# Two holds on early side work in a decoder block: squares of x's rows, and the first weights of the FFN

## The chip, the core and the metric

The kernel runs on one core of a Trainium2 chip. A core has five engines, each with its own instruction queue that is worked through in order: TensorE (PE in the profile, its weight loads PEld), VectorE (DVE), ScalarE (ACT), GpSimdE (POOL) and SyncE (SP), which here mostly issues DMAs. [...] The metric is the device time of one execution in microseconds.

## The reference, cut to what matters

One layer of a hybrid decoder, for x of 2048 rows by 1024 columns in float32:

```
hn   = rmsnorm(x, norm1_g)
u_pool, q, k, v = split(hn @ w_in)             # 512 columns each, 8 heads of 64
y_pool = ((mean of the last 2, 4, 8, 16 rows) - u_pool) @ pool_w * pool_scale
z = q k^T / 8, strictly causal;  log_a = log_sigmoid(z) + sum over later keys of log_sigmoid(-z)
y_attn = exp(log_a) @ v
h  = x + concat(rmsnorm(y_pool), rmsnorm(y_attn)) @ w_out
h  = h + relu(rmsnorm(h, norm2_g) @ w_up) ** 2 @ w_down      # 4096 hidden columns
y  = rmsnorm(h, final_g)
```

## The kernel before

The 2048 rows are treated as four blocks j = 0 to 3 of 512 rows; a tile holds 128 features by 512 rows. A float32 product is made from three passes in a reduced format: each operand is split into a high and a low part, `split` (L147 to L151), by a copy on ACT (L150) and a subtraction on DVE (L151), and `products` (L176 ff.) issues three matmuls per 128 features (L182 to L184). Weights come by DMA in the tile `raw` and are split five granules ahead of their use (`hl`, in `weights`, L167 ff.). A "chunk" is one such product of 128 output features by 512 rows over all 1024 inputs: 24 matmuls into one PSUM tile `pd`, of which there are two. What then takes the result out of `pd` is the chunk's evacuation.

The program has four stages in a row. The **front** runs for blocks 0 and 1 and again for 2 and 3: input projections, the pooling branch and the attention units, interleaved. For columns of v, `keep_v` (L488) copies `pd` to `vf`, for block 0 by a multiplication on DVE (L491) and for the others by a copy on ACT (L493), and PE transposes `vf` into `ptv` (L496). Beside this, `row_sums` (L382) makes the sums of squares that block 1 to 3's first norm needs: a quarter of a block's rows (512 KB) comes by DMA into the one tile `rlast` (L390), ACT squares it and sums along the row (L388), and only then the next quarter's DMA is issued. `sum_rows` (L395) takes one such step; in the front's second half it is noted once per chunk or two chunks.

The **output stage** (`tail`) multiplies by w_out, eight chunks c per block. `add_acc` (L878) adds `pd` to x on DVE (L881), sends the sum to memory as `hs` (L882) and notes its square for the second norm. At chunk 3 of the last block `begin_ffn` (L1605) opens the **FFN's** pools and takes the first step of `up`, a generator: it loads the first columns of w_up into `rb` (L986, 1 MB), makes weights from it (sums `rt` on DVE, L990 to L993, and splits `hw`), and makes the left operands (`make_left`: loads `sr`, 512 KB each, L1009, three buffers, so that load number i waits for the split of number i-3, and splits them into `sa`). The FFN uses a two-level fast matrix multiplication of seven products P1 to P7; in its first column PE does 12 matmuls each of P1 (tile `pY`), P2 (`pX`), P5 (`pZ`), then P6 and P7 (`pY` again). Before P6 can start, ACT copies P1's result out of `pY` (`p`, L1108). The **down** projection and the last norm follow.

The order of instructions on each engine isn't the order of the text: a scheduler puts the traced program in order by dependencies and a modelled timeline, and an instruction whose operands it takes to be ready early may stand far ahead of where it was written. A scope `tc.issue_after(ins)` forbids that: what is traced in it on the engine of `ins` is put behind `ins`. It adds no semaphore and binds no other engine. `last_split[0]` is the subtraction (DVE) of the weight split traced last, `done[1]` the evacuation of the chunk traced last, which is on DVE or ACT according to the chunk; for `add_acc` it is the addition on DVE.

Of the kernel before, what the change touches and what calls it, by code (L numbers as in the profile page):

```python
# [19 lines left out]
NT = S // T  # L20
# [25 lines left out]
def hymba_block(ctx: ExitStack, tc: tile.TileContext, xT, x_rows, gains, w_in, pool_w, w_out, w_up, w_down, out):  # L46
# [111 lines left out]
    raws, grans, last_split, last_mm, last_load = [], [], [None], [None], [None]  # L158
    done = [None, None]
# [145 lines left out]
    def make_h(j):  # L305
        return (hpb if j % 2 else hpa).tile([P, 2, T], F32R, tag="h", name="h", align_bytes=256)
# [18 lines left out]
    def step(n, emit, again=False):  # L325
        prog.append((n, emit, again))

    def note(emit):
        prog.append((0, emit, False))
# [53 lines left out]
    def row_sums(j):  # L383

        x = rlast.rearrange("p x t -> p (x t)")
        for b in range(TB + 1):
            if b:
                nc.scalar.activation(x, x, AF.Square, accum_out=sums1[:, j - 1, b - 1:b])  # L388
            if b < TB:
                nc.sync.dma_start(x, x_rows[j, b])  # L390
            yield

    row_steps = [iter(())] + [row_sums(j) for j in range(1, NT)]

    def sum_rows(j, n=1):  # L395
        for _ in range(n):
            next(row_steps[j])

    def norm1_rms(j):
        st[j]["ss"] = sums1[:, j - 1]  # L400
# [144 lines left out]
    def drained(j):  # L545
        while j not in finished:
            state["due"] = 0.0
            advance(0.1)
# [57 lines left out]
    def load_mix(j, n):  # L606
        st[j]["m"] = []
        for k in range(n):
            d = make_h(j)
            nc.sync.dma_start(d.bitcast(F32), mx[j][k].bitcast(F32))  # L610
            st[j]["m"].append((d[:, 0], d[:, 1]))

    def load_acc(j):
        acc = st[j]["acc"] = (bigp, accp, acc2p, acc3p)[j].tile([P, KD, T], F32, tag="big", name="acc")
        for k in range(0, KD, 2):
            nc.sync.dma_start(acc[:, k:k + 2], xT[j, :, k:k + 2])

    def tail(first):

        def root(j):  # L620

            if not (first and j < 2):
                drained(j)
                st[j]["todo"] = attn_norm(j, lambda: make_h(j))

        def mixes(j):
            load_mix(j, KD if first and j < 2 else 4)
            if "todo" in st[j]:
                st[j]["amix"] = st[j].pop("todo")()

        def begin(j):
            catch_up(len(later))
            st[j]["m"] += st[j].pop("amix", [])
            if j > 0:
                norm2(j - 1)
            if j == 2:
                sums_first()

        if first:
            note(to_out)  # L640
        else:
            note(lambda: (root(0), mixes(0), load_acc(0)))
        for j in range(NT):
            if j == 2 and first:
                note(to_last)
            note(lambda j=j: begin(j))
            for c in range(KD):
                if c == 0 and j == 0 and not first:
                    note(lambda: root(1))
                if c == 0 and j + 1 < NT:  # L650
                    note(lambda j=j: mixes(j + 1))
                if c == (2 if j == 0 else 4) and j + 2 < NT:
                    note(lambda j=j: root(j + 2))
                if c == 0 and j == 2:
                    note(lambda j=j: load_acc(j))
                if c == 4 and j in (0, 2):
                    note(lambda j=j: load_acc(j + 1))
                if c == 3 and j == NT - 1:
                    note(begin_ffn)
                wlist.append(w_out[c])  # L660
                step(2, lambda w, j=j, c=c: dense(j, "m", w, lambda ps: add_acc(j, c, ps)))

# [190 lines left out]
    def attn_norm(j, make=None):  # L853
        part = {}

        def load():

            if make:
                ol = [olp.tile([P, 2, T], F32, tag="ol", name="ol") for _ in range(2)]
            else:  # L860
                y = pa.tile([P, 4, T], F32, tag="yb", name="yb", bufs=1)
                ol = [y[:, 0:2], y[:, 2:4]]
            for i in range(2):
                nc.sync.dma_start(ol[i], os_[j][2 * i:2 * i + 2].rearrange("c p t -> p c t"))
            part.update({k: ol[k // 2][:, k % 2] for k in range(4)})

        if make:
            load()
        else:
            drained(j)  # L870
            later.append(load)
        return norm_parts(j, lambda k: part[k], ga, 4, make)
# [18 lines left out]
    def norm2(j):  # L891
        acc = [st[j]["acc"][:, k] for k in range(KD)]
        if j == 2:
            later.append(lambda: root_last(0, st[j]["sh"]))
        else:
            later_rms(st[j], "rh", lambda: st[j]["sh"], D)

        def put(k):
            nc.vector.scalar_tensor_tensor(acc[k], acc[k], g2[:, k:k + 1], st[j]["rh"], op0=ALU.mult, op1=ALU.mult)
        if j in PAIRS[0]:  # L900
            later.extend(lambda k=k: put(k) for k in range(KD))
# [12 lines left out]
    def sums_first():  # L914

        a, b = (st[j]["acc"] for j in PAIRS[0])

        def sums(c):
            lo, hi = slice(2 * c, 2 * c + 2), slice(4 + 2 * c, 6 + 2 * c)
            s1 = olp.tile([P, 2, T], F32, tag="sm", name="s1")  # L920
            nc.vector.tensor_tensor(s1, b[:, lo], b[:, hi], ALU.add)
            nc.vector.tensor_tensor(b[:, lo], a[:, lo], b[:, lo], ALU.subtract)
            s2 = olp.tile([P, 2, T], F32, tag="sm", name="s2")
            nc.vector.tensor_tensor(s2, s1, a[:, lo], ALU.subtract)
            for i, t in ((A11, a[:, lo]), (S2, s2), (A12, a[:, hi]), (S3, b[:, lo]), (S1, s1), (A22, b[:, hi])):
                nc.sync.dma_start(su[0][i][c], t)
            nc.vector.tensor_tensor(a[:, hi], a[:, hi], s2, ALU.subtract)
            nc.sync.dma_start(su[0][S4][c], a[:, hi])
        later.extend(lambda c=c: sums(c) for c in range(2))

    def up(pools, more):
# [49 lines left out]
        def load(q, m):  # L981
            if q and m % (NM // 2) == NM // 2 - 1:
                raw[q, m] = raw[0, m]
                return
            raw[q, m] = (rbb if m >= NM // 2 else rba).tile([P, 4, G, P], F32, tag="rb", name="rb")
            nc.sync.dma_start(raw[q, m], w_up[m])  # L986
# [9 lines left out]
        def make_weights(g):  # L996
            q, m, s = slots[g]
            which, i = what[s][1]
            if s == "P2":
                add_weights(q, m)  # L1000
            hl = hlp.tile([P, 2, G, P], F32R, tag="hw", name="hw", align_bytes=256)
            split((hl[:, 0], hl[:, 1]), (sums if which else raw)[q, m][:, i])
            ops[g] = hl
# [147 lines left out]
                    inner_sums(*waiting.pop(0))  # L1151

        load(*cols[0])
        make_weights(0)
        make_left(0, "P1")
        make_left(0, "P2")
# [9 lines left out]
        for g, (q, m, s) in enumerate(slots):  # L1166
# [7 lines left out]
            n = cols.index((q, m))  # L1174
# [19 lines left out]
            if g + UA < len(slots):  # L1194
                make_weights(g + UA)
                q2, m2, s2 = slots[g + UA]
                n = cols.index((q2, m2)) + 2
# [375 lines left out]
    def catch_up(n, stop=False):  # L1573
        for _ in range(n):
            if later[0] is None:
                later.pop(0)
                if stop:
                    return
                continue
            with ExitStack() as behind:  # L1580
                for ins in (last_split[0], done[0]):
                    if ins:
                        behind.enter_context(tc.issue_after(ins.ins))
                later.pop(0)()
# [21 lines left out]
    layer = []  # L1606

    def begin_ffn():
# [17 lines left out]
        layer.append(up([sap, hlp, rba, rtp, srp], more))  # L1626
        next(layer[0])

    def ffn():
        catch_up(len(later))  # L1630
        front_scope.close()
        for _ in layer.pop():
            pass
        left_scope.close()
        with ExitStack() as scope:
            spool = lambda name, bufs, **kw: scope.enter_context(tc.tile_pool(name=name, bufs=bufs, reuse_waits="tile", **kw))

            rlp, pupa = spool("rlp", 2), spool("pupa", 2)
            spool("even", 1).tile([P, 2 * P // 4], F32, name="even")
            rs = spool("rs", 2), spool("rs2", 3)  # L1640
            rt, t8 = spool("rt", 6), spool("t8", DA + 1)
            s8 = spool("s8", 2), spool("s82", 2 * DA - 1)
            tmp2, pup, rtx = spool("tmp2", 2), spool("pup", 6), spool("rtx", 1)
            down([t8, s8, rs, rt, pupa, pup, rtx, rlp, tmp2, spool("psb", 1, space=PS)])
# [20 lines left out]
    front(0)  # L1665
    front(1)
    tail(True)
    run()
    ffn()


# [62 lines left out]
```

## Time and profile before

| what | value |
|---|---|
| time, median of 3 runs | 1879.13 us (1877.73 to 1882.28) |
| the profiled execution | 1876.19 us, of which the span from the first to the last instruction is 1874.5 us |
| mean granted TensorE clock | 0.998 |
| PE busy | 1856.5 us, 99% of the span |
| DVE, ACT, POOL busy | 1458.1 us (78%), 1027.6 us (55%), 218.0 us (12%) |

The profile shows one execution. "Busy" is the time in which an engine had an instruction in work; matmuls overlap, so the step from one matmul's start to the next, not its duration, tells how fast PE goes. A row of a timeline gives start, duration, engine, line, operation, output and inputs, and in brackets how long the engine had been idle and whose end it waited for.

### The profile page before, as it was taken

To read this page: it belongs to the slowest core of one execution; us is meant where nothing else is said; L and a number is where in the kernel's file an instruction comes from. 1 tells how busy PE (TensorE), PEld (TensorE's weight loads), DVE (VectorE), ACT (ScalarE), POOL (GpSimd) and SP (SyncE) were. 2 spreads that over 40 slices of the span, in tenths; PEclk is the share of its full clock that TensorE was granted. 3 is DMA by queue.
4 is the path that set the end of the run, shared out by engine and by line. 5 is a ranking of instruction groups with operands and counts; after the bars stand their busy time and mean duration, and the time that the engine had idled before them with its cause. 6 is when DMAs were issued, how large, how long until landed. Compare 5 with 4: busy or idle time off the path is not lost.

```text
span 1874.5 us, 26609 instructions
## 1 busy us (share of the span) xinstructions
PE 1856.5 (99%) x8859; PEld 1549.6 (83%) x8859; DVE 1458.1 (78%) x2100; ACT 1027.6 (55%) x1620; POOL 218.0 (12%) x466
## 2 busy tenths in 40 slices
PE   9999999999999999999999999999999999999997
PEld 7888888888888788888888888887888888888887
DVE  6877798678866877887799988886665677889774
ACT  6655576466544555555566555554333665656643
POOL 1232232213311130000000000000010010020120
PEclk9999999999999999999999999999999999999999
DMA  7986786899796858978798988889999899999862
GB/s 274 300 269 208 232 295 212 272 338 301 271 371 239 303 181 311 342 279 306 277 355 300 330 295 279 284 303 336 375 325 333 272 319 305 331 304 349 287 214 92
DMA packets 223892, 542.20 MB, mean 289 GB/s; under 512 B 26240, under 2 KB 32384, under 8 KB 219904
## 3 DMA queue, kind: packets, MB, share of 16 engines
q1 hardware_dynamic: 218992, 531.75, 81.3%
q0 software_dynamic: 4608, 8.39, 2.5%
q8 instruction: 72, 1.18, 0.3%
q14 instruction: 76, 0.62, 0.1%
q10 hardware_dynamic: 144, 0.26, 0.0%
HBM read 355.75 MB, written 184.55 MB: 288 GB/s over the span
## 4 chain that ended last, share of the span: by engine, by line
PE 94%; DVE 2%; DMA 1%; ACT 1%; issue 0%; SPq 0%; POOL 0%; ACTq 0%; DVEq 0%
PE pY L1185 19%; PE pb L1358 16%; PE pb L1536 12%; PE pZ L1185 9%; PE pd L182 9%; PE pd L183 9%; PE pd L184 8%; PE pX L1185 5%; PE po L739 1%; PE pta L727 1%; PE pr L248 1%; PE pz L680 1%; PE pz L679 1%; PE pm L210 1%; PE pb L1476 0%
## 5 line engine op out<-in xcount | busy, mean ns | idle before, releaser
L1185 PE MATMUL pY<-sa,hw 128*128 128x512 f32 x1536 | 365.2, 389 | 0.7 <-ACT u L1108 0.7
L1185 PEld LDWEIGHTS pY<-sa,hw 128*128 128x128 f32 x1536 | 288.1, 188 | 60.9 <-ACT u L1108 1.1
L1358 PE MATMUL pb<-ad,wd 128*128 128x512 f32 x1344 | 304.8, 389 | 0.0
L182 PE MATMUL pd<-h,hl 128*128 128x512 f32 x752 | 295.1, 392 | 1.9 <-DVE acc L881 1.9
L1358 PEld LDWEIGHTS pb<-ad,wd 128*128 128x128 f32 x1344 | 252.3, 188 | 52.4
L184 PE MATMUL pd<-h,hl 128*128 128x512 f32 x752 | 295.4, 393 | 0.0
L183 PE MATMUL pd<-h,hl 128*128 128x512 f32 x752 | 295.1, 392 | 0.0
L1536 PE MATMUL pb<-ad,wd 128*128 128x512 f32 x1104 | 253.1, 390 | 1.1 <-ACT ad L150 1.0
L1536 PEld LDWEIGHTS pb<-ad,wd 128*128 128x128 f32 x1104 | 206.6, 188 | 44.5 <-ACT ad L150 1.5
L151 DVE TENSOR_TENSOR ad<-ar,ad 128x1024 fp32r<-128x1024 f32 x160 | 194.1, 1221 | 42.2 <-ACT ad L150 41.7
L150 ACT ACTIVATE ad<-ar 128x1024 fp32r<-128x1024 f32 x160 | 168.9, 1057 | 89.0 <-PE pb L1536 31.9
L1185 PE MATMUL pZ<-sa,hw 128*128 128x512 f32 x768 | 185.7, 389 | 0.0
L150 ACT ACTIVATE hl<-raw 128x512 fp32r<-128x512 f32 x168 | 105.6, 631 | 117.2 <-PE pd L184 108.1
L1185 PEld LDWEIGHTS pZ<-sa,hw 128*128 128x128 f32 x768 | 144.1, 188 | 29.9
L182 PEld LDWEIGHTS pd<-h,hl 128*128 128x128 f32 x752 | 141.3, 188 | 28.6 <-issue 2.3
L184 PEld LDWEIGHTS pd<-h,hl 128*128 128x128 f32 x752 | 141.3, 188 | 28.3
L183 PEld LDWEIGHTS pd<-h,hl 128*128 128x128 f32 x752 | 141.4, 188 | 26.8
L151 DVE TENSOR_TENSOR hl<-raw,hl 128x512 fp32r<-128x512 f32 x168 | 115.1, 688 | 44.6 <-ACT hl L150 44.0
L151 DVE TENSOR_TENSOR hw<-rt,hw 128x512 fp32r<-128x512 f32 x128 | 86.9, 687 | 36.0 <-ACT hw L150 35.8
L150 ACT ACTIVATE wd<-wq 128x1024 fp32r<-128x1024 f32 x56 | 59.5, 1063 | 80.4 <-PE pb L1358 71.6
L151 DVE TENSOR_TENSOR wd<-wq,wd 128x1024 fp32r<-128x1024 f32 x56 | 68.5, 1223 | 35.7 <-ACT wd L150 35.7
L1102 ACT ACTIVATE a<-a 128x512 f32<-128x512 f32 x96 | 59.9, 628 | 62.9 <-DVE a L1144 28.1
(235 smaller groups left out, 2684.0 us busy)
## 6 DMA issues: line engine op xcount, KB each, us to landing
ar<-sd SPq DMA_DIRECT2D x96, 512.0 KB, 5.7
ar<-sdi SPq DMA_DIRECT2D x64, 512.0 KB, 5.6
rb<-in_w_up_dram SPq DMA_DIRECT2D x30, 1024.0 KB, 6.9
sd<-a SPq DMA_DIRECT2D x104, 256.0 KB, 4.9
raw<-in_w_in_dram SPq DMA_DIRECT2D x50, 512.0 KB, 4.8
sdi<-hr SPq DMA_DIRECT2D x96, 256.0 KB, 5.4
wr<-in_w_down_dram SPq DMA_DIRECT2D x48, 512.0 KB, 5.7
sd<-s SPq DMA_DIRECT2D x88, 256.0 KB, 4.5
```

Source lines behind the costliest of these rows:

```text
L150: nc.scalar.activation(hi, src, AF.Copy)
L151: return nc.vector.tensor_tensor(lo, src, hi.bitcast(F32), ALU.subtract)
L182: nc.tensor.matmul(ps, hl[:, 0, c], hi, start=(k == 0), stop=False)
L183: nc.tensor.matmul(ps, hl[:, 0, c], lo, start=False, stop=False)
L184: last_mm[0] = nc.tensor.matmul(ps, hl[:, 1, c], hi, start=False, stop=(k == n - 1))
L210: marks["pm"] = nc.tensor.matmul(pm[:, c:c + 1], ss[:, c * P:(c + 1) * P], inv[n], start=(i == 0), stop=(i == len(parts) - 1))
L248: mm = nc.tensor.matmul(pr[:, b * P:(b + 1) * P], yr[:, x, b:b + 1].to_broadcast([P, P]), identr, start=(b == 0 and x == 0), stop=(b == TB ...
L679: nc.tensor.matmul(pz, qa[:, qsl], k, start=first, stop=False, skip_group_check=not (first and last))
L1102: nc.scalar.activation(t, src, AF.Relu)
L1185: nc.tensor.matmul(t, w[:, wx, c], a[:, ax, c % 2], start=first and c == 0 and x == 0, stop=last and c == G - 1 and x == 2, skip_group_che ...
L1358: nc.tensor.matmul(b, t[:, wx, 2 * (kk % 2) + c, i * P:(i + 1) * P], a[:, ax, c], start=p in ("P1", "P5", "P2") and kk == 0 and c == 0 and ...
L1536: nc.tensor.matmul(ps[q, n], block(t, wx, c, n), left_[q][:, ax, c], start=(n_ in ("P1", "P3") and kk == 0 and c == 0 and x == 0), stop=(n ...
```

## The change

Two holds are added, and one stop in the generator `up`. In `sum_rows`, a step taken singly is traced behind the latest weight split and the latest evacuation. In `up` a `yield` stands after the load of the first columns, so that `begin_ffn` at chunk 3 of the last block only opens the pools and issues that load; what it made besides (first weights, left operands) is now made by `later_ffn` at chunk 4, traced behind the latest split and the latest addition. No instruction is added or taken away.

```diff
@@ -394,7 +394,11 @@

     def sum_rows(j, n=1):
         for _ in range(n):
-            next(row_steps[j])
+            with ExitStack() as behind:
+                for ins in (last_split[0], done[1]):
+                    if ins and n == 1:
+                        behind.enter_context(tc.issue_after(ins.ins))
+                next(row_steps[j])

     def norm1_rms(j):
         st[j]["ss"] = sums1[:, j - 1]
@@ -657,6 +661,8 @@
                     note(lambda j=j: load_acc(j + 1))
                 if c == 3 and j == NT - 1:
                     note(begin_ffn)
+                if c == 4 and j == NT - 1:
+                    note(later_ffn)
                 wlist.append(w_out[c])
                 step(2, lambda w, j=j, c=c: dense(j, "m", w, lambda ps: add_acc(j, c, ps)))

@@ -1151,6 +1157,7 @@
                     inner_sums(*waiting.pop(0))

         load(*cols[0])
+        yield
         make_weights(0)
         make_left(0, "P1")
         make_left(0, "P2")
@@ -1626,6 +1633,10 @@
         layer.append(up([sap, hlp, rba, rtp, srp], more))
         next(layer[0])

+    def later_ffn():
+        with tc.issue_after(last_split[0].ins), tc.issue_after(done[1].ins):
+            next(layer[0])
+
     def ffn():
         catch_up(len(later))
         front_scope.close()
```

**On ACT in the front**, around the copy `vf` of block 1's v (L493, in the changed file L497). Squares are `rlast` (L388), `sh` and `sg` are an attention unit's, `at`, `ot`, `vt` and `mix` evacuations and splits. Before:

```order
L388 ACTIVATE rlast,sums_147<-rlast 128x1024
L150 ACTIVATE at<-pta 128x384
L696 ACTIVATE ot<-po 64x512
L150 ACTIVATE at<-pta 128x512
L388 ACTIVATE rlast,sums_147<-rlast 128x1024
L276 ACTIVATE r<-pr 128x512
L150 ACTIVATE vt<-ptv 128x8x64
L150 ACTIVATE hl<-raw 128x512
L388 ACTIVATE rlast,sums_147<-rlast 128x1024
L493 ACTIVATE vf<-pd 128x512
L150 ACTIVATE hl<-raw 128x512
```

and now:

```order
L276 ACTIVATE r<-pr 128x512
L150 ACTIVATE hl<-raw 128x512
L150 ACTIVATE vt<-ptv 128x8x64
L497 ACTIVATE vf<-pd 128x512
L388 ACTIVATE rlast,sums_147<-rlast 128x1024
L150 ACTIVATE hl<-raw 128x512
L702 ACTIVATE ot<-po 64x512
L150 ACTIVATE at<-pta 128x384
L150 ACTIVATE vt<-ptv 128x8x64
L150 ACTIVATE mix<-nt 128x512
L388 ACTIVATE rlast,sums_147<-rlast 128x1024
```

The three squares that stood before `vf` are gone; those of block 3 now stand far behind, from place 166 on, and the last two of block 2 stand behind `vf`, one of them straight behind it and one in front of an attention unit's `sh`.

**On DVE in the output stage of the last block**, from just after the addition of chunk 1, before:

```order
L151 TENSOR_TENSOR hl<-raw,hl 128x512
L992 TENSOR_TENSOR rt<-rb 128x512
L151 TENSOR_TENSOR hw<-rb,hw 128x512
L991 TENSOR_TENSOR rt<-rb,rt 128x512
L151 TENSOR_TENSOR hw<-rb,hw 128x512
L194 TENSOR_TENSOR sslast<-sslast,sq 128x512
L151 TENSOR_TENSOR hl<-raw,hl 128x512
L993 TENSOR_TENSOR rt<-rb,rt 128x512
L151 TENSOR_TENSOR sa<-sr,sa 128x1024
L218 TENSOR_SCALAR v<-pm 128x4
L151 TENSOR_TENSOR hw<-rt,hw 128x512 x3
L881 TENSOR_TENSOR acc<-pd,acc 128x512
```

and now, from that addition on (L881 is L887 here, L990 is L996):

```order
L887 TENSOR_TENSOR acc<-pd,acc 128x512
L151 TENSOR_TENSOR hl<-raw,hl 128x512
L194 TENSOR_TENSOR sslast<-sslast,sq 128x512
L151 TENSOR_TENSOR hl<-raw,hl 128x512
L218 TENSOR_SCALAR v<-pm 128x4
L887 TENSOR_TENSOR acc<-pd,acc 128x512
L151 TENSOR_TENSOR hl<-raw,hl 128x512
L194 TENSOR_TENSOR sslast<-sslast,sq 128x512
L151 TENSOR_TENSOR hl<-raw,hl 128x512
L887 TENSOR_TENSOR acc<-pd,acc 128x512
L151 TENSOR_TENSOR hw<-rb,hw 128x512
L151 TENSOR_TENSOR sa<-sr,sa 128x1024 x3
```

Before, the addition of chunk 2 is the last row, behind the first weights; now the additions of chunks 2 and 3 (second and third L887) stand ahead of all `hw`, `sa` and `rt`. Between the addition of chunk 3 and that of chunk 4 there now are `hw` twice, `sa` three times and `rt`, `hl` and `sslast` five times in all, and between those of chunks 4 and 5 three `sa`, two `rt`, two `hl` and one `sslast`.

**On ACT at the first columns of the FFN**, up to the copy `p` of P1 (L1108, now L1114), before:

```order
L150 ACTIVATE sa<-sr 128x1024
L193 ACTIVATE sq<-acc 128x512 x2
L150 ACTIVATE sa<-sr 128x1024
L193 ACTIVATE sq<-acc 128x512
L150 ACTIVATE sa<-sr 128x1024 x2
L150 ACTIVATE hw<-rb 128x512
L150 ACTIVATE hw<-rt 128x512
L1108 ACTIVATE p_8013<-pY 128x512
```

and now:

```order
L150 ACTIVATE hw<-rt 128x512 x3
L150 ACTIVATE sa<-sr 128x1024 x2
L193 ACTIVATE sq<-acc 128x512 x3
L150 ACTIVATE sa<-sr 128x1024 x3
L150 ACTIVATE hw<-rb 128x512
L150 ACTIVATE hw<-rt 128x512
L1114 ACTIVATE p_8013<-pY 128x512
```

Three left operands `sa` now stand straight before the two splits `hw` and the copy, where two stood before. On SP the load `rb` of those weights now follows straight behind the load `sr` of the eleventh operand; before, two sends of `hs` stood between them. Behind `rb` come the loads of the last three operands in both.

## Rows read from the trace of the kernel before

**Rows 1.** The page's first part: busy time, share of the span, instructions by engine.
```profile
PE 1856.5 (99%) x8859; PEld 1549.6 (83%) x8859; DVE 1458.1 (78%) x2100; ACT 1027.6 (55%) x1620; POOL 218.0 (12%) x466
```
**Rows 2.** The waits of PE: line, releaser, us in total, times, longest.
```profile
PE pd L182 <- DVE acc L881: 1.9, 1, 1.9
...
PE ptv L496 <- ACT vf L493: 1.5, 1, 1.5
```
**Rows 3.** A table by stretch: length, busy PE, PEld, DVE, ACT, POOL, granted clock, DMA.
```profile
110.00:120.00 10.00, 8.13 (x49) 6.79 (x48) 2.72 (x5) 4.76 (x9) 0.00 (x0) 1.00 0.60 194
650.00:660.00 10.00, 9.58 (x42) 7.96 (x43) 9.92 (x14) 5.81 (x8) 9.09 (x12) 1.00 0.81 272
```
**Rows 4.** Timeline of ACT, 106 to 120 us: start, duration, instruction, idle before.
```profile
106.58 1.06 ACT L388 ACTIVATE rlast<-rlast 128x1024 f32<-128x1024 f32 x1 [3.42 <-DMA rlast<-in_x_rows_dram]
...
117.88 1.06 ACT L388 ACTIVATE rlast<-rlast 128x1024 f32<-128x1024 f32 x1 [2.15 <-DMA rlast<-in_x_rows_dram]
...
118.93 0.58 ACT L493 ACTIVATE vf<-pd 128x512 f32<-128x512 f32 x1
```
**Rows 5.** Timeline of DVE, 108 to 111 us.
```profile
108.14 0.56 DVE L151 TENSOR_TENSOR at<-pta,at 128x384 fp32r<-128x384 f32 x1 [1.78 <-ACT at L150]
...
110.09 0.68 DVE L491 TENSOR_TENSOR vf<-pd,r 128x512 f32<-128x512 f32 x1
```
**Rows 6.** Timeline of PE at the two transposes of vf.
```profile
110.83 0.66 PE L496 MATMUL ptv<-ident,vf 128*128 128x128 f32 x4 [0.37 <-DVE vf L491]
...
119.56 0.66 PE L496 MATMUL ptv<-ident,vf 128*128 128x128 f32 x4 [1.50 <-ACT vf L493]
```
**Rows 7.** The tile rlast: who waited for its loads; issue to landing.
```profile
  ACT rlast L388: 12.9, 6
...
DMA to landing us min/median/max: 3.6/5.6/9.4
```
**Rows 8.** Timeline of DVE in the output stage, 636 to 655 us.
```profile
636.77 0.69 DVE L881 TENSOR_TENSOR acc<-pd,acc 128x512 f32<-128x512 f32 x1 [0.76 <-PE pd L184]
641.15 0.69 DVE L990 TENSOR_TENSOR rt<-rb 128x512 f32<-128x512 f32 x1 [3.69 <-DMA rb<-in_w_up_dram]
...
649.59 0.68 DVE L881 TENSOR_TENSOR acc<-pd,acc 128x512 f32<-128x512 f32 x1
650.20 2.35 DVE L151 TENSOR_TENSOR sa<-sr,sa 128x1024 fp32r<-128x1024 f32 x2
652.46 1.28 DVE L151 TENSOR_TENSOR hl<-raw,hl 128x512 fp32r<-128x512 f32 x2
653.67 0.68 DVE L194 TENSOR_TENSOR sslast<-sslast,sq 128x512 f32<-128x512 f32 x1
```
**Rows 9.** Timeline of PE, 648 to 651 us: end of chunk 3, start of chunk 4.
```profile
648.13 0.39 PE L184 MATMUL pd<-h,hl 128*128 128x512 f32 x1
650.42 0.47 PE L182 MATMUL pd<-h,hl 128*128 128x512 f32 x1 [1.91 <-DVE acc L881]
```
**Rows 10.** Timeline of PE at the FFN's first columns.
```profile
672.31 2.88 PE L1185 MATMUL pY<-sa,hw 128*128 128x512 f32 x12
675.03 2.88 PE L1185 MATMUL pX<-sa,hw 128*128 128x512 f32 x12
...
681.40 2.89 PE L1185 MATMUL pY<-sa,hw 128*128 128x512 f32 x12
```
**Rows 11.** DMA issues from 633 to 637 us: KB each, median us to landing.
```profile
sr<-su SPq DMA_DIRECT2D x3, 512.0 KB, 10.5
```
**Rows 12.** DMA issues from 647 to 662 us.
```profile
sr<-su SPq DMA_DIRECT2D x6, 512.0 KB, 4.4
```
**Rows 13.** Timeline of SP: the second load of w_up.
```profile
668.16 0.42 SPq L986 DMA_DIRECT2D rb<-in_w_up_dram  x1
```
**Rows 14.** The tile rb: issue to landing of its 30 loads.
```profile
DMA to landing us min/median/max: 4.9/6.9/9.2
```
**Rows 15.** Timeline of ACT: the copy of P1.
```profile
676.78 0.58 ACT L1108 ACTIVATE p<-pY 128x512 f32<-128x512 f32 x1
```

## The prediction

> **What bounds the kernel.** The page's first part comes first: PE is busy for 1856.5 of the 1874.5 us of the span [rows 1]. So a change can only gain where PE stands still, and it loses where it makes PE wait; what DVE, ACT or the DMAs do otherwise is free. The second view is therefore the list of what PE waited for. Three of its rows lie where this change moves something: 1.5 us at a transpose of vf that waited for ACT and 1.9 us at a chunk that waited for an addition on DVE to free its PSUM tile [rows 2], and 0.37 us at a transpose that waited for DVE [rows 6]. That is all there is to gain: under 4 us of 1876.
>
> [...]
>
> **The front, what goes.** ACT works its queue in order. At 117.88 a square of x's rows starts after ACT has stood idle for 2.15 us for the rows' DMA; vf stands behind it and starts at 118.93 [rows 4], and its transpose on PE at 119.56, after 1.50 us without work [rows 6]. In the new order no square stands between vf and the splits before it, so vf runs when its chunk ends and the 1.50 us go. The 0.37 us have the same source one step further: the square at 106.58 waited 3.42 us, the split of at behind it came late, DVE waited 1.78 us for that split, and DVE's vf stood behind it, at 110.09 [rows 4 to 6]. This square moves far back too, so 0.37 us go. Gain: 1.87 us.
>
> **The front, what comes.** The six squares that waited are only moved: each still needs a load of 512 KB into the one tile rlast, and the load is issued when the square before it is done. Issue to landing took 3.6 to 9.4 us, 5.6 at the median [rows 7]. In the new order three squares follow another closely: the last of block 2 with five ACT instructions between, two of block 3 with four and six. Five at about 0.6 us, as vf took [rows 4], cover 3.0 of 5.6 us, so ACT will stand some 2.6 us at each of the three, 0.6 at the shortest landing and 6.4 at the longest. The holds bind ACT only where the latest evacuation is an ACT instruction; that the latest split is on DVE does nothing for ACT or SP. Queued behind that square are an attention unit's sh and sg; after them GpSimd masks sg, DVE goes on with it, and PE transposes the result (pta). What this can cost PE: nothing, if the units ahead keep PE busy; at most what the old waits did. Those were 12.9 us of ACT [rows 7] and cost PE 1.87 us; 3 x 2.6 = 7.8 us by the same share are 1.1 us. A gain below nothing is excluded, since no other PE gap lies there. I take 0.5 us, between the free end and the share, because the old waits hit a copy with a transpose right behind it and the new ones hit units with several steps between; both ends, 0 and 1.9, stay for the range.
>
> **The output stage, what goes.** Twelve matmuls from 672.31 to 675.03 [rows 10] give 0.227 us per matmul and 5.44 us per chunk. Chunk 3's last matmul starts at 648.13, so chunk 4 could start at 648.36; it starts at 650.42 [rows 9]: 2.06 us lost. It waited for the tile that chunk 2 filled (end about 643.1, 24 matmuls before 648.5). DVE had no time for that addition: after chunk 1's at 636.77 it stood 3.69 us before rt for the load of w_up, worked through thirteen more operations, and came to the addition at 649.59 [rows 8]. In the new order only splits, a small sum and squares of the second norm stand ahead of it. One of these waits for an ACT square behind two weight splits that also wait for the load landing at 641.1, so I put the addition at 644.2; it is needed by 648.36, and chunk 3's follows at 648.6. The 2.06 us go.
>
> **The output stage, what is late next.** DVE now does the moved work between additions. A 512-wide operation steps by 0.605 us (two from 652.46 to 653.67), a split of sa by 1.13 (two from 650.20 to 652.46) [rows 8]. From 648.6: the addition, two hw, three sa, two rt, two hl and one sslast are eight short ones and three long, 8 x 0.605 + 3 x 1.13 = 8.2, so chunk 4's addition starts at 656.8 and is done at 657.5; chunk 6 needs the tile at 659.24 (648.36 + 2 x 5.44). Spare: 1.7 us. Then that addition, two rt, two hl, one sslast and three sa, 6 x 0.605 + 3 x 1.13 = 7.0: chunk 5's addition at 663.8, done at 664.5, needed by chunk 7 at 664.68. Spare: 0.2 us. Some of these steps also wait for ACT's half of a split, so I take 0.3 us of new stall, with 0 and 0.5 as near ends and the third rival as the far one.
>
> **The first columns of the FFN.** They start at 670.1 instead of 672.31. P6 comes 9.09 us after P1 (672.31 to 681.40 [rows 10]), at 679.2, and needs ACT's copy of P1, which before ran at 676.78 [rows 15], 4 us early. Now the copy comes later and P6 earlier. Behind the addition of chunk 5 DVE does three hw (to 666.2), the seventh sa, an addition, the eighth sa (to 669.1). Then the eleventh load sr may leave, and the load rb straight behind it at about 669.5, where it left at 668.16 [rows 13]. With the median of 6.9 us to landing it is there at 676.4, with the longest, 9.2, at 678.7 [rows 14]. Two splits and the copy add 1.6 us (from the copy's 0.58 [rows 15] and as much for each split, which overlap a little): 678.0 or 680.3 against 679.2. So 0 to 1.1 us; I take 0.3, near the median. The rest of the kernel gets the same instructions in nearly the same order, with PE's order unchanged: nothing.
>
> **Sum.** -1.87 - 2.06 + 0.5 + 0.3 + 0.3 = -2.8 us, from the profiled execution's 1876.19 to 1873.4. The median of the runs lies 2.94 us above that execution; carried over, the forecast is 1876.3 us, a gain of 0.15%.
>
> **Rivals.**
> First, the output stage gives half of its gain back: rb lands late, the copy of P1 stalls P6 by 1.1 us and chunk 5's addition is 0.5 us late. -1.87 - 2.06 + 0.5 + 0.5 + 1.1 = -1.8, so 1877.3. For it: 0.2 us of spare on DVE, and a copy behind a load. Against it: the median landing leaves 1.2 us.
>
> Second, the hold doesn't do what it says in the front: the squares are moved from one waiting place to others that cost the same 1.87 us. Then only the output stage counts, -2.06 + 0.6 = -1.5, so 1877.7. For it: the hold binds neither DVE's nor SP's queue and the rows are loaded no earlier relative to their squares. Against it: what stands behind the squares now.
>
> Third, slower. The first three loads of sr took 10.5 us to landing [rows 11], six later ones 4.4 [rows 12]. The fourth needs the buffer of the first: the first sa is now done at about 651.0 (648.6, an addition and an hw of 0.605, and 1.13). If it takes 10.5 us, it is there at 661.5, ACT's split ends at 662.6, and DVE, which was ready at 658.0, stands 4.6 us; chunk 5's addition starts at 668.4 and chunk 7 waits 4.4 us. -1.87 - 2.06 + 0.5 + 0.3 + 4.4 = +1.3, so 1880.4. It decides from a landing of about 9.3 us on (5.95 are covered, 0.2 spare, 3.1 are the gain to be lost). Against it: the slow three came together with 1 MB of w_up and the 256 KB of hs, and the fourth comes when no such load is under way. [...]
>
> **Chances.** Forecast 0.55, first rival 0.18, second 0.12, third 0.10, something that these views don't show 0.05. About 0.3%, 5.6 us, is what a measurement of this kernel can tell from no change. All four named cases lie within it, so faster by more needs more than the whole 3.9 us that the waits hold: 0.08; slower by more needs several of the losses at once: 0.06; within: 0.86. The range is 1872.8 to 1881.2: below, all of the 3.9 us without a new cost (1875.2) and 2.4 more, as three runs of one kernel spread over 4.5; above, the third rival and 0.8 more.
>
> **What would show it.** In the profile after: no wait of ptv for vf in the front, and no square ahead of vf on ACT; about three waits of 2 to 3 us of ACT for rlast behind 115 us; chunk 4 of the last block straight behind chunk 3; additions of chunks 4 and 5 at 8.2 and 7.0 us after the one before; the first pY 2.1 us earlier relative to chunk 3. Wrong would be: pta or po waiting over 1 us between 118 and 135 us; chunk 7 waiting for its tile; the second pY of the FFN waiting for p; or a granted clock under 1.00 in either stretch.

## The result and the profile after

The changed kernel took 1886.33 us (median of 6 runs, 1885.35 to 1890.09) against 1879.07 us of the kernel before (1876.67 to 1882.28): a ratio of 1.0045, 95% interval 1.0035 to 1.0055. The forecast was 1876.3 us with a range up to 1881.2: it is slower, by 7.3 us between the medians and 8.5 us by the ratio, and clear of the bound of 0.3% named in the prediction.

The first part of the page and two rows of its second part (40 slices of 47 us; tenths of busy time, tenths of the full clock):

```profile
PE 1859.9 (99%) x8859; PEld 1550.8 (82%) x8859; DVE 1458.9 (77%) x2100; ACT 1028.1 (55%) x1620; POOL 213.5 (11%) x466
...
PE   9999999999999989999999999999999999999997
...
PEclk9999999999999989999999999999999999999999
```

PE's sum has hardly changed [rows 1], but one slice in the middle, the fifteenth, has lost a tenth in both rows. The waits of PE (line, releaser, us in total, times, longest) name the place:

```profile
PE pr L248 <- POOL yrlast L894: 6.8, 1, 6.8
...
PE pZ L1192 <- ACT sa L150: 1.5, 1, 1.5
```

The two rows of [rows 2] are gone, as forecast. In their place stands one wait of 6.8 us that no part of the prediction spoke of: a transposition pr (L248) that waits for yrlast, which GpSimd makes. yrlast holds the root of the second norm of the last two blocks; eight transpositions per block spread it over the partitions. The timeline of PE there (start, duration, instruction, idle before):

```profile
684.24 1.00 PE L248 MATMUL pr<-identr,yrlast 128*128 128x128 f32 x8
685.08 0.67 PE L1192 MATMUL pX<-sa,hw 128*128 128x512 f32 x2
692.56 0.47 PE L248 MATMUL pr<-identr,yrlast 128*128 128x128 f32 x1 [6.81 <-POOL yrlast L894]
692.84 5.22 PE L1192 MATMUL pY<-sa,hw 128*128 128x512 f32 x12
697.90 2.48 PE L1192 MATMUL pX<-sa,hw 128*128 128x512 f32 x10
...
711.10 0.89 PE L248 MATMUL pr<-identr,yrlast 128*128 128x128 f32 x7
```

and that of the kernel before at the same work:

```profile
686.85 1.00 PE L248 MATMUL pr<-identr,yrlast 128*128 128x128 f32 x8
687.70 0.67 PE L1185 MATMUL pX<-sa,hw 128*128 128x512 f32 x2
688.21 2.88 PE L1185 MATMUL pY<-sa,hw 128*128 128x512 f32 x12
690.93 2.43 PE L1185 MATMUL pX<-sa,hw 128*128 128x512 f32 x10
...
704.07 1.00 PE L248 MATMUL pr<-identr,yrlast 128*128 128x128 f32 x8
```

Before, all eight transpositions of the last block stand at 704.07. Now one of them stands alone at 692.56, straight behind two matmuls of pX, and the other seven at 711.10. For the 6.81 us that this one waited, PE ran none of the matmuls behind it. The twelve pY and what lay between them took 5.06 us (692.84 to 697.90) where twelve took 2.72 us before (688.21 to 690.93): the clock. The table by stretch (length, busy PE, PEld, DVE, ACT, POOL, granted clock, DMA):

```profile
680.00:685.00 5.00, 5.00 (x28) 4.24 (x26) 5.00 (x8) 4.50 (x6) 3.70 (x1) 1.00 0.88 322
685.00:690.00 5.00, 0.75 (x5) 0.32 (x3) 3.83 (x6) 2.63 (x6) 4.67 (x5) 0.74 0.34 129
690.00:695.00 5.00, 2.44 (x6) 2.03 (x7) 0.00 (x0) 0.00 (x0) 1.99 (x11) 0.50 0.00 0
695.00:700.00 5.00, 5.00 (x18) 3.90 (x17) 1.27 (x2) 1.66 (x3) 0.00 (x0) 0.73 0.00 0
```

The granted clock is 0.50 from 690 to 695 us and comes back in the next stretch (0.73). So this place costs 6.8 us of standing and 2.3 us at half clock: 9.1 us together. By the starts of the rows it is 9.6 us: from the two pX to the ten pX PE took 12.82 us (685.08 to 697.90) where it took 3.23 before (687.70 to 690.93); this also counts the transposition itself, at half clock, and the last step ahead of the gap. The comparison of each kernel's n-th matmul shows it in one number: at the start of the FFN the changed kernel was 2.7 us ahead of the one before (669.63 against 672.31 [rows 10]); at the last matmul it is 9.4 us behind. Of these 12.1 us this place holds some 9.5, the wait of pZ for sa at 994 us 1.5 to 1.8, and smaller waits the rest.

The difference is in the order of PE. Behind the small products pm of the last block, before:

```
L1185 MATMUL pZ<-sa,hw 128x512 x8
L1185 MATMUL pY<-sa,hw 128x512 x24
L248 MATMUL pr<-identr,yrlast 128x128 x8
L1185 MATMUL pX<-sa,hw 128x512 x2
L1185 MATMUL pY<-sa,hw 128x512 x12
L1185 MATMUL pX<-sa,hw 128x512 x10
L1185 MATMUL pY<-sa,hw 128x512 x24
L1185 MATMUL pZ<-sa,hw 128x512 x24
```

and now:

```
L1192 MATMUL pZ<-sa,hw 128x512 x11
L1192 MATMUL pY<-sa,hw 128x512 x24
L248 MATMUL pr<-identr,yrlast 128x128 x8
L1192 MATMUL pX<-sa,hw 128x512 x2
L248 MATMUL pr<-identr,yrlast 128x128
L1192 MATMUL pY<-sa,hw 128x512 x12
L1192 MATMUL pX<-sa,hw 128x512 x10
L1192 MATMUL pY<-sa,hw 128x512 x24
L1192 MATMUL pZ<-sa,hw 128x512 x24
```

Straight behind the last line of each list stand the other transpositions of the last block, eight before and seven now. One transposition has moved ahead of 70 matmuls, while the steps of GpSimd that make its operand have not moved with it. It isn't the only difference: laid side by side, the two orders of PE differ in at least 19 places, 13 in the front between 87 and 238 us and six in the FFN between 678 and 815 us. The other five in the FFN cost at most some tenths: from matmul 3,700 (713 us in the kernel before) to matmul 4,800 the changed kernel stays 6.9 us behind. GpSimd's timeline after, first the root of another block, then this one:

```profile
641.40 0.20 POOL L219 TENSOR_SCALAR v<-v 128x4 int32<-128x4 int32 x1 [48.77 <-DVE v L218]
...
681.30 7.58 POOL L219 TENSOR_SCALAR v<-v 128x4 int32<-128x4 int32 x1 [34.61 <-DVE v L218]
...
692.32 0.19 POOL L894 CAST yrlast<-v 128x4 fp32r<-128x4 f32 x1
```

The same first instruction (L219, 128x4) takes 0.20 us at 641.40 and 7.58 us at 681.30. DVE over this time:

```profile
681.06 0.15 DVE L218 TENSOR_SCALAR v<-pm 128x4 f32<-128x4 f32 x1
681.13 0.68 DVE L996 TENSOR_TENSOR rt<-rb 128x512 f32<-128x512 f32 x1
...
687.54 1.28 DVE L151 TENSOR_TENSOR hw<-rt,hw 128x512 fp32r<-128x512 f32 x2
698.73 0.69 DVE L1134 TENSOR_TENSOR a<-pZ,u 128x512 f32<-128x512 f32 x1 [9.90 <-ACT u L1114]
```

From 681.13 to 688.8 DVE is busy without a break, with subtractions that read both operands from SBUF; GpSimd's instruction ends at 688.88, when DVE has nothing left. Before it was the same with 6.38 us, and it mattered to nobody, since PE asked for yrlast only at 704.07.

The steps that the prediction did work out came as said. DVE in the output stage, the additions of chunks 2 to 5 (they answer to [rows 8]):

```profile
642.55 0.69 DVE L887 TENSOR_TENSOR acc<-pd,acc 128x512 f32<-128x512 f32 x1 [1.24 <-PE pd L184]
...
647.99 0.69 DVE L887 TENSOR_TENSOR acc<-pd,acc 128x512 f32<-128x512 f32 x1 [1.36 <-PE pd L184]
...
656.22 0.69 DVE L887 TENSOR_TENSOR acc<-pd,acc 128x512 f32<-128x512 f32 x1
...
663.23 0.69 DVE L887 TENSOR_TENSOR acc<-pd,acc 128x512 f32<-128x512 f32 x1
```

and ACT in the front, with no square ahead of vf (against [rows 4]):

```profile
115.41 0.60 ACT L497 ACTIVATE vf<-pd 128x512 f32<-128x512 f32 x1 [2.10 <-PE pd L184]
115.90 1.05 ACT L388 ACTIVATE rlast<-rlast 128x1024 f32<-128x1024 f32 x1
...
121.37 1.06 ACT L388 ACTIVATE rlast<-rlast 128x1024 f32<-128x1024 f32 x1 [0.66 <-DMA rlast<-in_x_rows_dram]
```

### The profile page after: what moved, and what is told of

Read it like the earlier page. It is cut to its first block, busy times and chain, and to the rows that moved or that the text cites. A ratio compares the mean times of both kernels' runs of the same rounds, so it can differ in the third digit from the quotient of the medians.

```text
span 1884.0 us, 26608 instructions
## 1 busy us (share of the span) xinstructions
PE 1859.9 (99%) x8859; PEld 1550.8 (82%) x8859; DVE 1458.9 (77%) x2100; ACT 1028.1 (55%) x1620; POOL 213.5 (11%) x466
## 4 chain that ended last, share of the span: by engine, by line
PE 83%; DMA 6%; DVE 6%; issue 2%; ACT 2%; POOL 1%; SPq 0%; DVEq 0%; ACTq 0%; POOLq 0%
PE pY L1192 16%; PE pb L1365 14%; PE pb L1543 12%; PE pZ L1192 8%; PE pd L182 7%; PE pd L183 7%; PE pd L184 7%; PE pX L1192 4%; PE po L745 1%; DMA ar<-sd 1%; PE pta L733 1%; DMA ar<-sdi 1%; PE pr L248 1%; DVE sa L151 1%; DMA os<-ot 1%
## 5 line engine op out<-in xcount | busy, mean ns | idle before, releaser
L1108 ACT ACTIVATE a<-a 128x512 f32<-128x512 f32 x96 | 60.0, 628 | 68.6 <-DVE a L1150 34.3
```

The source lines that it names most:

```text
L1108: nc.scalar.activation(t, src, AF.Relu)
```

## The experiments

Theory A: the whole loss is the one early transposition, with GpSimd's slow root and the half clock behind it, and it comes with the second part of the change. Rival B: the squares' hold carries part of it. Rival C: the FFN's weights and left operands are late, and the transposition only shows that.

**One part alone.** Only the hold on the squares (`part1_squares`):

```diff
-                if c == 4 and j == NT - 1:
-                    note(later_ffn)
...
         load(*cols[0])
-        yield
```

> Only the hold on the squares of x's rows; the FFN's first weights are made as before. Theory A (the loss is the early transposition of yrlast, which the second part brings): PE's order in the FFN is that of before, no wait of pr for yrlast, and the time is about 0.4 us under before (the n-th matmul of the changed kernel was 0.4 us ahead at 246 us), so 1878.7 us against 1879.1. Rival B (the squares' new waits, or a later clock, carry part of the loss): over 1881 us.

Measured: 1876.38 us (12 runs) against 1878.25 of before (29 runs), ratio 0.9991, interval 0.9981 to 1.0001. That is nearer to 2 us under the kernel before than to the 0.4 us expected, but the interval reaches 1. And only the second part (`part2_weights`):

```diff
-            with ExitStack() as behind:
-                for ins in (last_split[0], done[1]):
-                    if ins and n == 1:
-                        behind.enter_context(tc.issue_after(ins.ins))
-                next(row_steps[j])
+            next(row_steps[j])
```

> Only the yield and the later making of the FFN's first weights; the squares stand as before. Theory A: the same transposition is moved ahead, pr waits some 6.8 us for yrlast, twelve matmuls after it run at half clock (2.35 us), and the time is the changed kernel's plus 0.4 us, 1886.7. Rival B: under 1883 us.

Measured: 1887.07 us, ratio 1.0047 (1.0032 to 1.0061). Its first rows among the waits of PE are the new one and, since the squares stand as before, the old ones of vf:

```profile
PE pr L248 <- POOL yrlast L890: 6.5, 1, 6.5
PE ptv L496 <- ACT vf L493: 1.7, 1, 1.7
```

PE's order in the FFN is that of the kernel before, matmul for matmul, in the first of these runs, and that of the changed kernel in the second. So the loss is in the second part alone, and rival B falls.

**The transposition put back.** The changed kernel with one more hold on PE (`hold_spread`; `part2_hold` is the same without the squares' hold):

```diff
-                    nc.tensor.matmul(t, w[:, wx, c], a[:, ax, c % 2], ...
+                    mm = nc.tensor.matmul(t, w[:, wx, c], a[:, ax, c % 2], ...
...
-                spread(pr, yrlast[:, i])
+                with tc.issue_after(mm.ins) if i else nullcontext():
+                    spread(pr, yrlast[:, i])
```

> The changed kernel with one more hold: the eight transpositions of the last yrlast are put behind the matmuls of their slot on PE, so the one that had moved ahead goes back to the other seven. Theory A: the wait of pr (6.81 us) and the stretch at half clock (2.35 us) go, 1886.3 - 9.2 = 1877.1 us, about 2 us under before. Rival C (what is late is the weights and left operands, and the transposition only shows it): another instruction waits in its place and the time stays over 1884 us.

Measured: 1877.16 us (12 runs), ratio 0.9993 (0.9983 to 1.0003).

> Only the later making of the FFN's first weights, with the transpositions held back as in the run beside it. Theory A: 1877.5 us, 0.4 over the run with both parts. Rival C: over 1884 us. If the two parts do not add up (this one at or under the run with both), the squares' hold is worth nothing.

Measured: 1876.17 us (11 runs), ratio 0.9989 (0.9981 to 0.9998). GpSimd's root is as slow as ever and harms nobody; here is the run with both parts, GpSimd and PE:

```profile
682.65 7.58 POOL L219 TENSOR_SCALAR v<-v 128x4 int32<-128x4 int32 x1 [33.47 <-DVE v L218]
```

```profile
687.28 3.04 PE L1192 MATMUL pY<-sa,hw 128*128 128x512 f32 x12 [0.34 <-ACT u L1114]
690.16 2.43 PE L1192 MATMUL pX<-sa,hw 128*128 128x512 f32 x10
```

Where the early transposition stood, the twelve pY now take 2.9 us to the next pX, near the 2.7 us of before. Theory A named 1877.1 us, and the weights and left operands are as late in this kernel as in the changed one: rival C falls. The hold also brought four places further back in the FFN (733 to 815 us) to their order of before; in the changed kernel PE lost nothing there, as said above. The gains of the two parts do not add up: the one with both is not ahead of the one without the squares' hold. Each of the three kernels without the early transposition (`part1_squares`, `hold_spread`, `part2_hold`) lies within a few tenths of a per cent of the kernel before, which is also what these runs can tell apart.

**The transposition moved in the kernel before.** (`early_in_before`; the tiles pr are made ahead, as `prs`.)

```diff
+            if g == 5:
+                prs[1] = psu.tile([P, T], F32, tag="R", name="pr")
+                ahead = spread(prs[1], yrlast[:, 1], 0, 1)
             for c in range(G):
...
-                    nc.tensor.matmul(t, w[:, wx, c], ...
+                    with tc.issue_after(ahead[0].ins) if g == 5 else nullcontext():
+                        nc.tensor.matmul(t, w[:, wx, c], ...
```

> The kernel before, with nothing changed but the place of one transposition: the first of the last yrlast is put on PE behind 62 matmuls of the FFN (about 15 us behind its start), some 70 matmuls ahead of the other seven; some matmuls of the second column change places with it. Theory A (the early transposition alone costs the time): yrlast is ready at 691.0 us, PE would reach it at about 687.2, so pr waits 3 to 4 us, and the time is 1878.2 + 3.7 = 1882 us, or 1884 if the half clock follows this gap too. Rival (the early place does harm only together with the moved weights and left operands): under 1880 us.

Measured: 1883.13 us (10 runs) against 1878.61, ratio 1.0024 (1.0013 to 1.0035), without any of the change.

```profile
689.96 0.47 PE L249 MATMUL pr<-identr,yrlast 128*128 128x128 f32 x1 [2.88 <-POOL yrlast L890]
690.24 5.43 PE L1191 MATMUL pY<-sa,hw 128*128 128x512 f32 x12
695.46 1.28 PE L249 MATMUL pr<-identr,yrlast 128*128 128x128 f32 x8
```

```profile
690.00:695.00 5.00, 5.00 (x12) 3.98 (x13) 0.00 (x0) 0.00 (x0) 0.19 (x1) 0.50 0.15 56
```

A gap of 2.9 us, and behind it the twelve matmuls take 5.2 us instead of 2.7, at a granted clock of 0.50. So the early place does the harm by itself, and the clock fell with this shorter gap as well. The loss of 0.24% is under the prediction's bound of 0.3%, though its interval excludes none; it is these rows that carry the argument. The time lies between the expectation's two figures, 1882 and 1884. The gap is shorter than assumed because PE came to the transposition later: 15.7 us behind the FFN's start (671.39) where 14.9 were assumed, while yrlast came 18.5 us behind it, as in the kernel before (18.6).

**Still earlier in the changed kernel** (`early_in_after`): the same edit on top of the change.

> The changed kernel with the early transposition another 12 matmuls earlier, about 12 us behind the FFN's start, at about 681.8 us. Theory A: yrlast is ready at 692.5 as before, so the wait grows from 6.8 to at most 10.7 us, and the stretch at half clock stays; 1886.3 + 3.9 = 1890 us. Less if the standing PE lets DVE run dry sooner and GpSimd with it. Rival C: no change from 1886.3 us.

Measured: 1888.44 us (4 runs), ratio 1.0057 (1.0041 to 1.0074). The wait of pr did not grow:

```profile
668.55 2.88 PE L1198 MATMUL pY<-sa,hw 128*128 128x512 f32 x12
...
683.48 0.73 PE L1198 MATMUL pX<-sa,hw 128*128 128x512 f32 x2 [2.63 <-ACT hw L150]
691.05 0.48 PE L249 MATMUL pr<-identr,yrlast 128*128 128x128 f32 x1 [6.84 <-POOL yrlast L896]
```

```profile
680.00:685.00 5.00, 1.58 (x6) 0.67 (x4) 5.00 (x9) 4.41 (x8) 4.59 (x1) 1.00 0.99 348
```

The place in the order alone doesn't set the price. Of the 2.7 us by which twelve matmuls fewer should bring PE sooner to the transposition, 2.6 went to another wait of this order, pX for a weight split: PE stood before pr from 15.7 us behind the FFN's start on, against 16.1 in the changed kernel. And yrlast was ready 22.5 us behind that start instead of 22.9, since DVE ran out of work 0.4 us sooner and GpSimd's first instruction ended with it, at 687.4. The upper bound of 10.7 us was a miss: the condition under "less" came, but is worth 0.4 us, and the wait of pX, which the expectation did not name, the rest. The row of the table says one thing more: the gap of 2.6 us ahead of pX left the granted clock at 1.00.

**GpSimd let in.** Six instructions on DVE that read PSUM and write a tile nobody uses, traced behind the root's first step (`psum_ops_on_dve`; shortened). The edit also traces both roots at high priority, so that the scheduler places work anew here too:

```diff
-        y = inv_root(mean_squares([ss], D, where, tag), nc.gpsimd)
+        pm = mean_squares([ss], D, where, tag)
+        with tc.high_priority():
+            y = inv_root(pm, nc.gpsimd)
+            if i:
+                for _ in range(6):
+                    nc.vector.tensor_scalar(junk, pm (repeated over 512 columns), 1.0, 0.0, ...
```

> The changed kernel with six more instructions on DVE (512 columns, 0.6 us each, read from PSUM, written to a tile that nothing uses), the first right behind DVE's step of the last root, the others spread over the following ten; PE's early transposition moves to a harmless place by itself. The question is GpSimd's first instruction of that root (L219), which took 7.58 us in the changed kernel, until DVE had nothing to do, and 0.20 us for another block. Theory A (GpSimd stands as long as DVE reads two operands from SBUF): it ends during the first added instruction, 0.2 to 0.8 us, and the steps after it end in the later ones. Rival (it is slow by itself, after 34 us without work): 6 to 8 us again. The time: no wait of pr, 1877 to 1879 us, in spite of 3.6 us more work on DVE.

Measured: 1875.72 us (10 runs), ratio 0.9983 (0.9973 to 0.9992), a little under the 1877 to 1879 expected. GpSimd and DVE in this kernel:

```profile
680.86 0.19 POOL L219 TENSOR_SCALAR v<-v 128x4 int32<-128x4 int32 x1 [33.71 <-DVE v L218]
681.13 0.20 POOL L226 TENSOR_TENSOR v<-v 128x4 f32<-128x4 f32 x1
681.41 2.35 POOL L227 TENSOR_TENSOR v<-v 128x4 f32<-128x4 f32 x1
...
684.41 3.43 POOL L226 TENSOR_TENSOR v<-v 128x4 f32<-128x4 f32 x1
...
688.48 1.77 POOL L229 TENSOR_TENSOR v<-v 128x4 f32<-128x4 f32 x1
```

```profile
680.68 0.69 DVE L898 TENSOR_SCALAR junk<-pm 128x512 f32<-128x512 f32 x1
...
683.62 0.69 DVE L898 TENSOR_SCALAR junk<-pm 128x512 f32<-128x512 f32 x1
...
687.69 0.69 DVE L898 TENSOR_SCALAR junk<-pm 128x512 f32<-128x512 f32 x1
...
690.09 1.42 DVE L898 TENSOR_SCALAR junk<-pm 128x512 f32<-128x512 f32 x2
```

The first instruction now takes 0.19 us. Each of the next long ones ends some 0.15 us behind the start of an added instruction: 681.41 + 2.35 = 683.76 with one at 683.62, 687.84 with 687.69, 690.25 with 690.09. GpSimd was not slow by itself; it was kept out. In these traces DVE's subtractions of two SBUF operands kept it out, and an instruction that reads PSUM let it in. The other root in the changed kernel shows the same: beside the addition of chunk 2 at 642.55, which reads PSUM, three of its steps (642.52, 642.80, 643.08) took 0.20 us each, and beside the split hl at 644.20, with two SBUF operands, one took 0.74 us (644.21 to 644.95). Between the ten such subtractions in a row from 681.13 on, GpSimd did not get in once in 7.6 us. Why they exclude each other was not shown. PE in this kernel:

```profile
691.67 0.33 PE L248 MATMUL pr<-identr,yrlast 128*128 128x128 f32 x1
```

The root as a whole was hardly sooner: yrlast was ready at 691.6, 22.4 us behind the FFN's start against 22.9 in the changed kernel, since three of its later steps were kept out in turn. What freed the time is PE's order: one transposition still stands ahead of the other seven (691.67 against 701.91), but 26 matmuls further back, where yrlast was just ready. So this run shows what kept GpSimd's instructions; its time is that of a kernel without the wait, and not the price of a slow root.

## Why the prediction was wrong

The step that failed is one sentence: "The rest of the kernel gets the same instructions in nearly the same order, with PE's order unchanged: nothing." PE's order was not unchanged. It differed at 19 places or more, and at one of them one of 8,859 matmuls had moved ahead by 70, to a place where its operand was not ready; that cost some 9 us, more than twice all that the change could gain. New and old orders were compared for ACT, DVE and SP, and not for PE, the engine that bounds the kernel. The three rivals looked at DVE, at ACT, at loads and at the copy of P1, and none at GpSimd, though its root ends in a PE operand. None of the prediction's own signs of being wrong came either: no wait of pta or po over 1 us from 118 to 135 us, no wait of chunk 7 or of the second pY, and a clock of 1.00 in both stretches of [rows 3].

Step by step:

- The front, what goes (1.87 us): right. Both waits of ptv for vf are gone.
- The front, what comes: smaller waits than said. ACT stood for rlast 3.0 us in three waits from 80 to 260 us instead of 7.8, since the loads landed in 4.2 to 4.8 us; but PE lost some time at other places of the front (0.2 to 0.3 us each). At 246 us the changed kernel was 0.4 us ahead, where 1.4 were forecast. This is one execution against one. By PE's 1,300th matmul (255 us) the five profiles with the squares' hold are 0.3 to 1.5 us ahead of the kernel before, and the three without it lie between 0.7 us ahead and 2.0 us behind: the forecast fits within this spread, which doesn't settle it.
- The output stage, what goes (2.06 us): right; chunk 4 follows chunk 3 at once.
- What is late next: right to the tenth. The additions stand 8.2 and 7.0 us apart (647.99, 656.22, 663.23), and no chunk waited for its tile. The third rival did not come: the fourth load of sr landed in 3.3 us, the two behind it in 4.5 and 4.7 us.
- The copy of P1: it ran at 678.16 for a P6 at 678.74, at the very edge; the same copy cost 0.4 us in the run with the second part alone. Forecast 0 to 1.1.
- The rest: wrong, as above. With that one instruction put back, the kernel takes 1877.16 us (0.9993 of the kernel before, where 0.9985 was forecast), inside the range.
- The clock: the sum counts each gap at its own length, with nothing behind it. The clock of 1.00 in [rows 3] bore that out for gaps of 1.5 and 1.9 us, and `early_in_after` for one of 2.6; it did not hold for 2.9 and 6.8, where the clock stood at 0.50 behind the gap and the twelve matmuls there took 2.3 to 2.5 us more. The rows looked at were only of short gaps. From 20 to 1870 us of the changed kernel no other stretch of 10 us shows a clock under 1.00, in the output stage, where the two tiles pd take turns, as little as elsewhere.

What stays open: why the scheduler moved one of the eight and not the others. It goes with the second part of the change and not with the first. And of the 2.8 us forecast net gain some 1 to 2 us appear in the runs with the transposition put back, in `hold_spread` not clear of noise; in the profile of the one with both parts other small waits of PE have come in, pY for u (1.2 us) and pd for qk (1.2 us) the longest; whether these belong to the change or to one execution was not tried. A part of it does not belong to the change: from its 6,000th matmul to the last every other profile loses 0.7 to 2.1 us against that of the kernel before, and `early_in_before`, which has nothing of the change, loses most.

## What to carry to other kernels

When a change lets a scheduler place work anew, compare the whole order of the engine that bounds the kernel, not only that around the edit, and for each instruction that moved ahead look up in the trace when its operand is ready. Here PE paid for one early instruction with 6.8 us in which nothing behind it ran. The root on GpSimd, beside a DVE that worked through subtractions of two SBUF operands, ended when DVE let it in (its first instruction took up to 7.6 us instead of 0.2), not after the sum of its durations: leave it slack. Giving it to another engine was not tried.

## What the runs showed of the hardware

The first 128x4 instruction of GpSimd's root took 0.19 to 0.20 us where DVE read PSUM or stood idle, and 6.4 to 7.6 us beside DVE subtractions of two SBUF operands in a row, until the first break. TensorE's clock stayed at 1.00 over gaps of 1.5 and 1.9 us (the kernel before) and 2.6 us (`early_in_after`); it stood at 0.50 behind gaps of 2.9 us (`early_in_before`) and 6.8 us (the changed kernel, `early_in_after`) for some 5 us of matmuls, which cost a further 2.3 to 2.5 us. And six useless instructions on DVE, 3.6 us of work, went with a time about 11 us under the changed kernel's (0.9983 against 1.0045 of the kernel before): the wait was gone, because the transposition had moved 26 matmuls back.
